# Output product of the attention half by token block, and the half weights of the last feed-forward output asked for one by one

## The chip, the cores and the metric

The program runs on one core of one Trainium2 chip. The metric is the device time of one launch in microseconds (us); lower is better. The kernel before takes 2506.91 us as the median of three runs, 2506.32 to 2507.97.

## What is computed

One layer of a streaming encoder for 1088 tokens: 1024 of a new stream and 64 of a running one, model width 1024, all in float32. A feed-forward half step and a layer norm come first, then two attention branches from one projection, then the part that the change touches, then a second feed-forward half step and a layer norm:

```python
h = _layer_norm(alpha * x + 0.5 * _swiglu(x, ffn1_wi, ffn1_wo), ln1_g, ln1_b)
oa, ob, ga, gb, states = mixer(h)
ya = oa.reshape(b, t, WIDTH_A) @ w_branch_a
yb = ob.reshape(b, t, WIDTH_B) @ w_branch_b
mix = (jax.nn.sigmoid(ga) * ya + jax.nn.sigmoid(gb) * yb) @ w_out
h = _layer_norm(alpha * h + mix, ln2_g, ln2_b)
h = _layer_norm(alpha * h + 0.5 * _swiglu(h, ffn2_wi, ffn2_wo), ln3_g, ln3_b)
```

`w_out` is 1024 x 1024. Its product and the second layer norm are called the output stage below.

## The kernel before

**Tiles.** Features lie on the 128 partitions, tokens along the free axis, so the width of 1024 is eight feature tiles (`KT` = 8, index `d` or `k`). The tokens are three blocks of 384, 384 and 320 (`TB`, index `b`).

**Products in three.** Every operand is split into a high and a low float32r part, and a product of one feature tile is three matmuls (high by high, high by low, low by high; `mm3`, line 495). One product of the output stage is `(d, b)`: 8 input tiles times 3 = 24 matmuls into one PSUM bank.

**Weights.** A chunk of weights (here 128 x 1024, 512 KB: all that is needed for one `d`) is loaded by a DMA on the SP queue into one of two raw buffers (`wr`; `dma_upto`, line 382), and split (`split_next`, line 395): ACT copies the high part into a weight slot, then DVE, or POOL where the chunk carries the flag `pool`, subtracts it to give the low part. There are two slots, `w_s0` and `w_s1`. A slot is free again when the last matmul of its chunk is done; a raw buffer when the low part of its chunk is done, and then the load of the chunk after the next is issued. `add` (line 458) makes one job of a chunk: get the weights, split the next chunk ahead, run the products of the blocks that it is given, release.

**The output stage.** `to_out` (line 2394) allots the result tiles `Y2` (`y2_d`, all tokens of one feature tile). `out_of(d, b, w)` (line 2410) takes a tile of `h` that was loaded from memory (`ask_h`, line 2337, three ahead), runs the product, and DVE forms `y = alpha * h + product`; from the second `d` on a running sum `acc` over the feature tiles is kept (`add_up`, line 816; for the last block it lies in a tile named `c`). After `d` = 7 of a block `norm2` plans its layer norm (`layer_norm`, line 532): a matmul with ones gives the mean; DVE subtracts it from the eight `y` (eight rows `y<-y,b`, called centring here); ACT or DVE squares; DVE or POOL adds the squares (`lns`, `lnq`); matmuls of one column give the variance; ACT and DVE give `rstd`; transposes spread it over the partitions; DVE scales (eight rows `y<-y,lnp,b`); the bias is added; and ACT, DVE and POOL form the high and low parts of the factors of the second feed-forward half (`A11`, `A12`, and from the second half of the tokens `S3`, `A22`).

Before the change the jobs are: for each `d`, blocks 0 and 1; then for `d` = 0 to 6 block 2, with the flag `pool` on every other chunk; then `last_out` (line 2428) with `(7, 2)`, which also starts the loads of the second feed-forward half and plans the norm of block 2.

**What sets the order.** `Plan` (line 131) holds a model of each engine's time and emits the instructions of the vector engines in the order in which that model says they can start, while PE's order is that of the jobs, with the norm's matmuls put in between. Each engine then works strictly through its own list, and waits on semaphores where an operand is missing. So a row that is late holds up every row behind it on its engine.

**The last output of both feed-forward halves.** `last_outputs` (line 1269) multiplies the last four hidden tiles by eight half chunks `l0` to `l7` (`get_unit`, line 979, makes sure that the split of one is planned). Before the change all eight are asked for ahead of the first product.

All vector instructions have line 120 of the profile, because one wrapper issues them; rows are told apart by their tiles.

Of the kernel before, what the change touches and what calls it, by code (L numbers as in the profile page):

```python
# [34 lines left out]
KT = D // P  # L35
# [8 lines left out]
NF = DFF // P  # L44
# [286 lines left out]
def tile_trunk(ctx, tc, a):  # L331
# [92 lines left out]
    def get(i):  # L424
        while st["split"] <= i:
            split_next()
        w, t = hls[i]
        plan.until(lambda: t.end is not None)
        return w

    def ahead(i):

        while st["split"] <= min(i, len(chunks) - 1) and free_slot() is not None:
            split_next()

    def release(i):
        finished[i] = plan.t["pe"]
        hls.pop(i)
# [19 lines left out]
    def add(ap, fn, cols=1024, pool=False, blocks=(0, 1, 2)):  # L458
        c = len(chunks)
        chunks.append((ap, cols, pool))  # L460

        def run():
            w = get(c)
            ahead(c + 1)
            for b in blocks:
                fn(b, w)
            release(c)
        jobs.append(run)
# [347 lines left out]
    def add_up(ACC, Y, d, b, n, tmp):  # L816

        def add(e):
            if d == 1:
                ACC[b] = tmp.tile([P, 384], F32, name="acc", tag="acc", bufs=2)  # L820
            other = Y[0, b] if d == 1 else ACC[b]
            of(e).tensor_tensor(ACC[b][:, :n], other[:, :n], Y[d, b][:, :n], op=OP.add)
        if d:
            summed[b] = plan.task(adders(n), "acc", add, [summed[b]] if d > 1 else (), 2, None, [Y[d, b]])
# [55 lines left out]
    def add_ffn7(wi, wo, wl, G, gi, put, beside_it, last, end):  # L880
# [93 lines left out]
        def some():  # L974
            while G.hold and at.next < len(units):
                prepare()
        G.some = some

        def get_unit(kind, f):
            i = by[kind, f]  # L980
            while at.next <= i:
                prepare()
            plan.until(lambda: units[i].t.end is not None)
            return units[i]
# [5 lines left out]
        def wait(*tasks):  # L990
            plan.until(lambda: all(t.end is not None for t in tasks))
# [147 lines left out]
        def out_products(fs, d, b, w, off):  # L1139

            n = TB[b]
            p = bank("mm")
            mm3(p, w, [F[f].h[:, :, TO[b]:TO[b] + n] for f in fs], n, off)
            y = Y[d, b]
            if (d, 0, 0) not in touched:
                wait(*G.read[d])
                nc.vector.scalar_tensor_tensor(y, y, ALPHA, p[:, :n], op0=OP.mult, op1=OP.add)
            else:
                nc.vector.tensor_tensor(y, y, p[:, :n], op=OP.add)
# [119 lines left out]
        def last_outputs():  # L1269
            fs = list(range(NF - 4, NF))  # L1270
            wait(*(F[f].t[x, s] for f in fs for x in ("h1", "h2") for s in range(2)))
            last()
            st["solo"] = False
            some()
            us = [get_unit(f"l{d}", NF) for d in range(KT)]
            for b in range(3):
                if b:
                    G.next_weights()
                for d in range(KT):
                    wait(*(outs[d, half, s, 0] for half in range(1 + (b > 0)) for s in range(2)))  # L1280
                    skip = 2 * (d < 2)
                    out_products(fs[skip:], d, b, us[d].slot, skip)
                    if gi == 2 and b == 2:
                        last_norm(d, b, Y, ACC, G.tmp, G.room, put)
                    else:
                        add_up(ACC, Y, d, b, TB[b], G.tmp)
                    if b == 2:
                        G.freed(us[d].home)
                if gi < 2 or b < 2:
                    layer_norm(b, [Y[k, b] for k in range(KT)], ACC, gi, G.tmp, put, G.room(b) if gi == 2 else None)  # L1290
# [36 lines left out]
        for x, fs in order:  # L1327
            for f in fs:
                if x == "plain":
                    f, half = f  # L1330
# [34 lines left out]

        jobs.extend(steps)
        jobs.append(last_outputs)
        jobs.append(end)

# [950 lines left out]
    def fetch(order, tag, bufs, load):  # L2320

        order, ready = list(order), {}

        def ask(key):
            while key not in ready or (order and len(ready) < bufs):
                x = order.pop(0)
                n = TB[x[1]]
                ready[x] = load(x[0], x[1], n)
            return ready.pop(key)
        return ask  # L2330
# [3 lines left out]
        nc.sync.dma_start(h[:, :n], h_d[d * P:(d + 1) * P, TO[b]:TO[b] + n])  # L2334
        return h

    ask_h = fetch([(d, b) for d in range(KT) for b in (0, 1)] + [(d, 2) for d in range(KT)], "or", 3, load_h)

    gate_order = [(d, b) for d in range(6) for b in range(3)] + [(d, b) for b in range(3) for d in (6, 7)]
    GT, gated = {}, {}  # L2340
# [69 lines left out]
    def out_of(d, b, w):  # L2410
        n = TB[b]
        h = ask_h((d, b))
        p = bank("mm")
        mm3(p, w, have_m(b), n)
        nc.vector.scalar_tensor_tensor(Y2[d, b], h[:, :n], ALPHA, p[:, :n], op0=OP.mult, op1=OP.add)
        add_up(ACC2, Y2, d, b, n, G2.tmp if b < 2 else Own)

    def norm2(b, tmp):
        layer_norm(b, [Y2[k, b] for k in range(KT)], ACC2, 1, tmp, put2)

    def f_out(d):
        def fn(b, w):
            out_of(d, b, w)
            if d == KT - 1:
                norm2(b, G2.tmp)
        return fn
# [57 lines left out]
        add(*br[d], cols=512)  # L2484
    add_joint(br[6:], cols=512)
    jobs.append(to_out)
    for d in range(KT):
        add(a["wout"][d], f_out(d), blocks=[0, 1])
    for d in range(KT - 1):
        add(a["wout"][d], f_out(d), blocks=[2], pool=d % 2 == 0)  # L2490
    chunks.append((a["wout"][KT - 1], 1024, False))
    jobs.append(last_out)

# [132 lines left out]
```

## Time and profile before

| | us |
|---|---|
| median of the runs | 2506.91 |
| the profiled execution | 2507.51 |
| its span, first to last instruction | 2505.7 |
| PE busy in the span | 2432.4 |
| PEld (weight loads into the array) busy | 2379.4 |
| DVE busy | 1752.6 |
| ACT busy | 1285.1 |
| POOL busy | 349.0 |

The output stage runs from 1639.9 us to 1748.1 us of the span, the norm of its last block to 1773 us. A row of a timeline gives the start, the time that it took, the engine, the tiles it writes and reads, how many instructions are merged in it, and in brackets how long the engine had been idle before it and what ended that. PEld is the clearest engine for gaps of TensorE: before each matmul its weights go into the array, and while PE is kept busy PEld is too. A granted clock (PEclk) of 1.00 is 2.4 GHz and 0.50 is 1.2 GHz.

### The profile page before, as it was taken

How to read it: one execution, taken by the hardware profiler on the slowest of the kernel's cores; microseconds unless marked ns; L12 is line 12 of the kernel's file. 1: busy time of each engine (PE TensorE's matmuls, PEld its weight loads, DVE VectorE, ACT ScalarE, POOL GpSimd, SP SyncE). 2: the span in 40 equal slices, each digit the busy share in tenths (PEclk: the TensorE clock that was granted, in tenths of full speed). 3: DMA queues.
4: the chain of work that ended last, by engine and by line, in shares of the span. 5: the costliest groups of instructions: out<-in, count | busy, mean ns of one | idle time of the engine just before them, and what ended most of it. 6: DMA issues, size and time to landing. Idle time of an engine off the chain costs nothing.

```text
span 2505.7 us, 46746 instructions
## 1 busy us (share of the span) xinstructions
PE 2432.4 (97%) x17338; PEld 2379.4 (95%) x17338; DVE 1752.6 (70%) x4246; ACT 1285.1 (51%) x2712; POOL 349.0 (14%) x477
## 2 busy tenths in 40 slices
PE   9999999999999999999999999999999999999995
PEld 9999999999998899999999998998999999999995
DVE  7666655666586889888676767657956665667758
ACT  5333333333345698777857777524633333343324
POOL 0000000000042222222243332314000000000004
PEclk9999999999999999999999999999999999999997
DMA  5466532273222322223221111643256643145322
GB/s 184 125 207 204 170 103 88 86 222 93 81 84 89 117 70 86 92 76 92 68 77 54 60 51 55 200 139 117 79 151 190 189 145 91 60 141 189 90 67 72
DMA packets 221204, 285.41 MB, mean 114 GB/s; under 512 B 20704, under 2 KB 146512, under 8 KB 220944
## 3 DMA queue, kind: packets, MB, share of 16 engines
q1 hardware_dynamic: 200864, 257.40, 33.4%
q10 hardware_dynamic: 19552, 22.81, 2.8%
q8 instruction: 136, 2.23, 0.4%
q0 software_dynamic: 560, 2.21, 0.2%
q14 instruction: 92, 0.75, 0.1%
HBM read 207.62 MB, written 75.00 MB: 113 GB/s over the span
## 4 chain that ended last, share of the span: by engine, by line
PE 76%; DVE 9%; ACT 8%; issue 3%; DMA 3%; POOL 1%; ACTq 0%; SPq 0%; DVEq 0%; POOLq 0%
PE b L120 76%; ACT w L120 2%; ACT scores L120 2%; DVE w L120 1%; DVE y L120 1%; DVE k L120 1%; ACT pt L120 1%; DMA g<-g_d 1%; DVE pt L120 1%; DVE scores L120 1%; DVE w_s L120 1%; ACT z L120 1%; DVE sc L120 0%; ACTq L120 0%; DMA st<-in_wo_dram 0%
## 5 line engine op out<-in xcount | busy, mean ns | idle before, releaser
L120 PE MATMUL b<-x,w_s 128*128 128x384 f32 (+1 forms) x3528 | 637.3, 332 | 6.3 <-ACT w_s L120 2.2
L120 PE MATMUL b<-A,w_s 128*128 128x272 f32 (+1 forms) x4824 | 633.1, 291 | 4.9 <-DVE y L120 1.8
L120 PEld LDWEIGHTS b<-A,w_s 128*128 128x128 f32 x4824 | 619.9, 189 | 9.4 <-ACT fac L120 2.1
L120 PEld LDWEIGHTS b<-x,w_s 128*128 128x128 f32 x3528 | 587.8, 189 | 15.2 <-ACT w_s L120 2.8
L120 PE MATMUL b<-S,w_s 128*128 128x272 f32 x4032 | 516.8, 288 | 3.0 <-ACT c L120 3.0
L120 PEld LDWEIGHTS b<-S,w_s 128*128 128x128 f32 x4032 | 509.0, 188 | 6.1 <-ACT c L120 4.4
L120 ACT ACTIVATE w_s<-wr 128x512 fp32r<-128x512 f32 (+1 forms) x345 | 227.4, 660 | 383.0 <-PE b L120 207.1
L120 DVE TENSOR_TENSOR w_s<-wr,w_s 128x512 fp32r<-128x512 f32 (+1 forms) x323 | 229.9, 714 | 143.8 <-ACT w_s L120 139.3
L120 PE MATMUL b<-fac,w_s 128*128 128x272 f32 x1800 | 228.2, 288 | 0.9 <-DVE y L120 0.9
L120 PEld LDWEIGHTS b<-fac,w_s 128*128 128x128 f32 x1800 | 226.8, 188 | 1.2 <-ACT fac L120 1.2
L120 POOL TENSOR_TENSOR w_s<-wr,w_s 128x256 fp32r<-128x256 f32 x196 | 149.6, 789 | 417.7 <-ACT w_s L120 170.5
L120 ACT ACTIVATE c<-b 128x272 f32<-128x272 f32 (+1 forms) x262 | 102.1, 391 | 97.2 <-PE b L120 88.9
L120 DVE TENSOR_TENSOR c<-c,b 128x272 f32<-128x272 f32 x240 | 103.4, 433 | 63.8 <-PE b L120 60.6
L120 POOL TENSOR_TENSOR lns<-lns,lnq 128x384 f32<-128x384 f32 (+1 forms) x25 | 27.1, 1084 | 739.2 <-ACT lnq L120 738.1
L120 DVE TENSOR_TENSOR pt<-b,pt 128x512 fp32r<-128x512 f32 (+4 forms) x184 | 96.5, 545 | 31.2 <-ACT pt L120 29.4
L120 POOL TENSOR_TENSOR y<-y,c 128x384 f32<-128x384 f32 (+1 forms) x15 | 17.3, 1174 | 706.0 <-DVE acc L120 691.3
L120 ACT ACTIVATE c<-c 128x272 f32<-128x272 f32 x160 | 69.0, 432 | 82.8 <-DVE c L120 80.4
L120 PE MATMUL b<-pt,v 128*128 128x256 f32 (+3 forms) x672 | 103.5, 281 | 4.9 <-DVE pt L120 2.3
L120 PEld LDWEIGHTS b<-pt,v 128*128 128x128 f32 (+1 forms) x672 | 93.5, 188 | 13.5 <-DVE pt L120 4.3
L120 ACT ACTIVATE w<-w,mx 128x640 f32<-128x640 f32 (+5 forms) x144 | 100.5, 698 | 10.4 <-DVE mx L120 7.6
L120 PE MATMUL b<-m,w_s 128*128 128x384 f32 (+1 forms) x576 | 100.4, 334 | 3.2 <-DVE w_s L120 2.6
L120 ACT ACTIVATE w<-w,sm 128x640 f32<-128x640 f32 (+5 forms) x144 | 97.7, 698 | 9.5 <-DVE sm L120 4.8
(274 smaller groups left out, 3235.5 us busy)
## 6 DMA issues: line engine op xcount, KB each, us to landing
wr<-in_wi_dram SPq DMA_DIRECT2D x156, 256.0 KB, 3.1
ff_d<-c SPq DMA_DIRECT2D x144, 136.0 KB, 2.9
a<-ff_d SPq DMA_DIRECT2D x72, 272.0 KB, 3.8
st<-in_wo_dram SPq DMA_DIRECT2D x72, 256.0 KB, 5.1
tw_d<-st SPq DMA_DIRECT2D x72, 256.0 KB, 2.6
wr<-in_wz_dram SPq DMA_DIRECT2D x35, 512.0 KB, 3.6
wr<-tw_d SPq DMA_DIRECT2D x48, 256.0 KB, 2.7
q<-in_wi_dram SPq DMA_DIRECT2D x39, 256.0 KB, 3.2
```

The source lines that it names most:

```text
L120: r = real(*args, **kw)
```

## The change

The output stage now goes by token block: all eight `d` of block 0, then all of block 1, then seven of block 2 and `last_out`. Each chunk of `w_out` is therefore loaded and split three times, 24 chunks in place of 16, and none of them carries the flag `pool` any more. The loads of `h` follow the new order. In `last_outputs` each half chunk is asked for just ahead of its first product.

```diff
@@ last_outputs
-            us = [get_unit(f"l{d}", NF) for d in range(KT)]
+            us = {}
             for b in range(3):
                 if b:
                     G.next_weights()
                 for d in range(KT):
+                    if not b:
+                        us[d] = get_unit(f"l{d}", NF)
                     wait(*(outs[d, half, s, 0] for half in range(1 + (b > 0)) for s in range(2)))
@@ the loads of h
-    ask_h = fetch([(d, b) for d in range(KT) for b in (0, 1)] + [(d, 2) for d in range(KT)], "or", 3, load_h)
+    ask_h = fetch([(d, b) for b in range(3) for d in range(KT)], "or", 3, load_h)
@@ the jobs of the output stage
     jobs.append(to_out)
-    for d in range(KT):
-        add(a["wout"][d], f_out(d), blocks=[0, 1])
-    for d in range(KT - 1):
-        add(a["wout"][d], f_out(d), blocks=[2], pool=d % 2 == 0)
+    for b in range(3):
+        for d in range(KT - (b == 2)):
+            add(a["wout"][d], f_out(d), blocks=[b])
     chunks.append((a["wout"][KT - 1], 1024, False))
     jobs.append(last_out)
```

What stands on the engines shows what moves. First PE, at the mean of block 0's norm (`acc..,ones`), before the change and then after it. The tiles `m0` to `m7` are the inputs, their second number is the block, `w_s0` and `w_s1` are the slots.

```order
L120 MATMUL b2_19926<-m2_1_19085,w_s0_19824 128x384 x3
L120 MATMUL b2_19926<-m3_1_19141,w_s0_19824 128x384 x3
L120 MATMUL b5_19940<-acc_19550,ones_132 128x384
L120 MATMUL b2_19926<-m4_1_19198,w_s0_19824 128x384 x3
L120 MATMUL b2_19926<-m5_1_19322,w_s0_19824 128x384 x3
```

```order
L120 MATMUL b0_19721<-m2_1_19085,w_s1_19684 128x384 x3
L120 MATMUL b0_19721<-m3_1_19141,w_s1_19684 128x384 x3
L120 MATMUL b5_19739<-acc_19524,ones_132 128x384
L120 MATMUL b0_19721<-m4_1_19198,w_s1_19684 128x384 x3
L120 MATMUL b0_19721<-m5_1_19322,w_s1_19684 128x384 x3
```

Before, this mean stands inside the last product of block 1 (the 16th product of the stage); now it stands inside the first product of block 1 (the 9th), so that norm has 15 products behind it where it had 8. The mean of block 1 stands in the first product of block 2 in both.

Next the SP queue behind the fourth chunk, before and after. `wr` is a chunk of weights, `h32` a tile of `h`.

```order
L120 DMA wr_19450<-in_wout_dram 128x1024
L120 DMA h32_19479<-h_d_71 128x384
L120 DMA h32_19509<-h_d_71 128x384
L120 DMA wr_19523<-in_wout_dram 128x1024
L120 DMA h32_19541<-h_d_71 128x384
```

```order
L120 DMA wr_19450<-in_wout_dram 128x1024
L120 DMA h32_19480<-h_d_71 128x384
L120 DMA wr_19495<-in_wout_dram 128x1024
L120 DMA h32_19514<-h_d_71 128x384
L120 DMA wr_19530<-in_wout_dram 128x1024
```

In blocks 0 and 1 each tile of `h` now has a chunk of weights ahead of it in the queue, where every second one had; in block 2 it was one to one already.

Last DVE, from the `y` of the last product `(7, 2)` towards the centring of block 2 (`y2_0<-y2_0,b5 128x320`), before and after. Rows of 160 and 384 columns belong to the norm of block 1.

```order
L120 SCALAR_TENSOR_TENSOR y2_7_19427<-h32_20218,b0_20309 128x320
L120 CAST A11_19428<-y2_0_19420 128x160
L120 TENSOR_TENSOR c_18677<-c_18677,y2_7_19427 128x320
L120 TENSOR_TENSOR A11_19428<-y2_0_19420,A11_19428 128x160
L120 TENSOR_TENSOR A11_19428<-y2_1_19421,A11_19428 128x160
L120 SCALAR_TENSOR_TENSOR y2_2_19422<-y2_2_19422,lnp_133,b7_20344 128x384
L120 SCALAR_TENSOR_TENSOR y2_3_19423<-y2_3_19423,lnp_133,b7_20344 128x384
L120 SCALAR_TENSOR_TENSOR y2_4_19424<-y2_4_19424,lnp_133,b7_20344 128x384
L120 CAST A11_19428<-y2_2_19422 128x160
L120 SCALAR_TENSOR_TENSOR y2_5_19425<-y2_5_19425,lnp_133,b7_20344 128x384
```

```order
L120 SCALAR_TENSOR_TENSOR y2_7_19427<-h32_20280,b0_20370 128x320
L120 CAST A12_19432<-y2_6_19426 128x160
L120 TENSOR_TENSOR c_18677<-c_18677,y2_7_19427 128x320
L120 TENSOR_TENSOR A12_19432<-y2_6_19426,A12_19432 128x160
L120 TENSOR_TENSOR A12_19432<-y2_7_19427,A12_19432 128x160
L120 TENSOR_TENSOR S3_20423<-y2_0_19420,S3_20423 128x224
L120 TENSOR_TENSOR w_s0_20429<-wr_20361,w_s0_20429 128x512 x2
L120 TENSOR_TENSOR S3_20423<-y2_1_19421,S3_20423 128x224
```

Between that `y` and the first centring row there are 26 instructions before the change and 14 after it. The 12 that are gone from there (six scalings, three low parts and two casts of 160 columns, one bias row) now stand ahead of the last product.

## Rows read from the trace of the kernel before

**Rows 1.** The page, part 1: busy us, share of the span and instructions of each engine.

```profile
PE 2432.4 (97%) x17338; PEld 2379.4 (95%) x17338; DVE 1752.6 (70%) x4246; ACT 1285.1 (51%) x2712; POOL 349.0 (14%) x477
```

**Rows 2.** Windows: stretch, length, busy PE, PEld, DVE, ACT, POOL, clock, DMA.

```profile
1641.00:1706.00 65.00, 64.94 (x369) 64.94 (x370) 27.31 (x43) 9.70 (x12) 4.72 (x6) 1.00 0.39 119
1706.00:1748.00 42.00, 36.82 (x229) 34.72 (x227) 38.02 (x67) 23.44 (x41) 22.22 (x23) 0.96 0.46 149
1748.00:1773.00 25.00, 20.67 (x135) 19.36 (x136) 20.00 (x52) 16.55 (x38) 1.54 (x3) 0.86 0.25 75
```

**Rows 3.** Timeline of PEld over the output stage and behind it.

```profile
1718.34 0.74 PEld L120 LDWEIGHTS b<-ones,lns 128*128 128x128 f32 x6 [1.70 <-POOL lns L120]
...
1733.31 6.75 PEld L120 LDWEIGHTS b<-m,w_s 128*128 128x128 f32 x46 [1.59 <-DVE w_s L120]
1740.94 0.30 PEld L120 LDWEIGHTS b<-m,w_s 128*128 128x128 f32 x2 [0.88 <-ACT w_s L120]
1742.20 0.59 PEld L120 LDWEIGHTS b<-m,w_s 128*128 128x128 f32 x4 [0.96 <-DVE w_s L120]
...
1745.77 0.30 PEld L120 LDWEIGHTS b<-ident,rstd 128*128 128x128 f32 x3 [0.55 <-issue]
...
1748.07 0.42 PEld L120 LDWEIGHTS b<-A,w_s 128*128 128x128 f32 x3 [1.13 <-ACT y L120]
...
1762.93 0.79 PEld L120 LDWEIGHTS b<-A,w_s 128*128 128x128 f32 x6 [1.53 <-ACT c L120]
1766.76 1.23 PEld L120 LDWEIGHTS b<-ones,lns 128*128 128x128 f32 x6 [3.04 <-issue]
```

**Rows 4.** Windows of 4 us, same columns, where the clock is below 1.00.

```profile
1720.00:1724.00 4.00, 4.00 (x19) 4.00 (x18) 3.86 (x8) 3.11 (x6) 0.53 (x1) 0.57 0.67 184
...
1764.00:1768.00 4.00, 1.21 (x6) 1.22 (x6) 3.56 (x8) 2.27 (x3) 0.00 (x0) 0.60 0.41 110
1768.00:1772.00 4.00, 4.00 (x20) 4.00 (x20) 0.30 (x2) 0.40 (x2) 0.00 (x0) 0.54 0.28 91
```

**Rows 5.** Timeline of DVE in block 2 and behind it.

```profile
1707.14 2.41 DVE L120 TENSOR_TENSOR y<-y,b 128x384 f32<-128x384 f32 x5 [1.61 <-PE b L120]
...
1731.23 2.02 DVE L120 TENSOR_TENSOR w_s<-wr,w_s 128x1024 fp32r<-128x1024 f32 x1
...
1740.92 1.23 DVE L120 TENSOR_TENSOR w_s<-wr,w_s 128x1024 fp32r<-128x1024 f32 x1 [1.15 <-ACT w_s L120]
...
1747.47 0.48 DVE L120 SCALAR_TENSOR_TENSOR y<-h,b 128x320 f32<-128x320 f32 x1
...
1748.89 1.66 DVE L120 SCALAR_TENSOR_TENSOR y<-y,lnp,b 128x384 f32<-128x384 f32 x3
...
1757.48 0.48 DVE L120 TENSOR_TENSOR y<-y,b 128x320 f32<-128x320 f32 x1
```

**Rows 6.** Instructions on the tile m: weight loads into the array.

```profile
L120 PEld LDWEIGHTS b<-m,w_s x576: 186/188/329, 1639.9 to 1746.7; 128*128 128x128 f32 x192
```

**Rows 7.** Timelines of ACT and SP: one split, and the load issued when it ended.

```profile
1649.47 1.06 ACT L120 ACTIVATE w_s<-wr 128x1024 fp32r<-128x1024 f32 x1 [3.72 <-PE b L120]
...
1651.82 0.33 SPq L120 DMA_DIRECT2D wr<-in_wout_dram  x1
```

**Rows 8.** The last chunk of the stage: its load's issue, ACT's row, and the load's landing.

```profile
1733.29 0.33 SPq L120 DMA_DIRECT2D wr<-in_wout_dram  x1
...
1739.83 1.06 ACT L120 ACTIVATE w_s<-wr 128x1024 fp32r<-128x1024 f32 x1 [1.55 <-DMA wr<-in_wout_dram]
...
DMA to landing us min/median/max: 6.5/6.5/6.5
```

**Rows 9.** DMA issues from 1640 to 1773 us: count, size, median us to landing.

```profile
wr<-in_wout_dram SPq DMA_DIRECT2D x16, 512.0 KB, 3.6
```

**Rows 10.** Last output of the second feed-forward half: the last half chunk on ACT and PE.

```profile
2430.30 0.63 ACT L120 ACTIVATE w_e<-wr 128x512 fp32r<-128x512 f32 x1 [2.77 <-DMA wr<-in_wl_dram]
...
2438.25 1.20 PE L120 MATMUL b<-h,w_e 128*128 128x384 f32 x6
```

## The prediction

> **What bounds the kernel now.** I read the page first: PE is busy for 97% of the span, so time can come only from the few places where TensorE stands still or runs at half clock [rows 1]. The windows by stage show where that is around the change. While blocks 0 and 1 are multiplied, PEld is busy 64.94 us of 65.00 and DVE 27.31: PE sets the pace, and DVE has room for more than as much again. In the 42 us in which block 2 is multiplied beside the norms of blocks 0 and 1, DVE is busy 38.02 and PEld only 34.72. In the 25 us behind, PEld is busy 19.36 [rows 2]. So the two norms that end together, at the end of block 1, crowd DVE, and TensorE pays.
>
> The timeline of PEld names the gaps [rows 3]. 1.70 us ahead of the variance matmuls of block 0's norm (`lns` came late from POOL, which at that time also did low parts of weights). 1.59 for a weight slot on DVE. 0.88 and 0.96 for the last chunk. 0.55 at the spreading of `rstd` of block 1. 1.13 for a factor of the second half. Then, behind the stage, 1.53 for ACT (`c`), and 3.04 ahead of the variance matmuls of block 2's norm. Their sum is 11.38 us. The clock adds to it: after the 1.70 gap it is 0.57 over 4 us, which with PE busy throughout costs 4 x 0.43 = 1.7. After the 3.04 gap it is 0.54 from 1768 to 1772, 4 x 0.46 = 1.8, and 0.50 for the 1.2 us before that in which PE worked, 0.6: together 2.4 [rows 4]. So 15.5 us lie in reach, 0.6% of the kernel. After 1773 PE goes on without such gaps, and what is won there stays won to the end.
>
> **The change part by part.** *Removed, 1.70 + 1.7.* Block 0's norm now begins in the first product of block 1. In that block DVE has eight centrings and eight `y<-h` at 0.48 each, eight scalings at 0.55 [rows 5], eight low parts of weights at 1.23 [rows 5], seven low parts of factors and ten additions at about 0.5 (my estimate from centrings of the same width), small rows of 1.3: 3.8 + 3.8 + 4.4 + 9.8 + 8.5 + 1.3 = 31.6 us. PE takes eight products of 24 x 0.1755 = 4.2 us (64.94 us for 370 loads [rows 2]), 33.7, plus 1.5 for the norm's own matmuls. It fits, tightly. And POOL, whose late row ended this gap, has lost the low parts of four chunks that stood between its additions. I take the whole gap, and the clock with it.
>
> *Removed, 1.59 + 0.55.* Before, block 2 carried centrings and scalings of two norms; now of one: by the same prices 3.8 + 3.8 + 4.4, seven low parts 8.6, and about 7 for the rest, 27.6 us beside 28.2 of products (24 x 0.147 = 3.5 each: 6.75 us for 46 loads [rows 3]) and 1.6 of other matmuls. Bounds: nothing of the two waits goes (DVE is still nine tenths full), or all. I take all, since the slot then has time: from ACT's start on a chunk to the load that waits for its low part are 2.35 us [rows 7], and a product lasts 3.5 or 4.2.
>
> *Removed in part, 0.9 of 1.84.* The last chunk was late for its load: issued at 1733.29, it took 6.5 us where the median is 3.6 [rows 8, 9], for the first loads of the feed-forward half follow it at once. They still do. But it is issued when the low part of the chunk two before is done, which stood just at the start of that chunk's product (PE went on at 1733.31 [rows 3]) and should now stand about 0.9 us ahead of it: 3.5 of a product less the 2.35 above and some 0.25 for two semaphores (my estimate). I take 0.9, between 0 and 1.84.
>
> *Removed, 1.53 + 3.04 + 2.4.* From the `y` of the last product to the first centring of block 2 DVE took 10.0 us, 1747.47 to 1757.48. Twelve of its 26 rows now stand earlier: six scalings, 3.3 us at 0.55 [rows 5], and six small rows that I estimate at 1.5. The centring comes 4.8 us earlier, at 1752.7 by this trace's time, and 9.3 us after it (1757.48 to 1766.76) the variance can begin: 1762.0. PE, without the two gaps, comes to it at 1766.76 - 3.04 - 1.53 = 1762.2. So both gaps go, by a hair, and PE itself is late next. The 1.53 wait is for ACT, whose row `c` stands behind squares of the same norm, which come earlier too. I take both, and the half clock after them. Bounds: 0 and 7.0.
>
> *Kept.* The 1.13 gap: the factors of block 1's last columns depend on a norm that still starts in the first product of block 2.
>
> *Added: eight chunks.* Eight loads of 512 KB on SP, eight ACT rows of 1.06 [rows 7], and twelve low parts on DVE, eight new and four that came from POOL. In block 0 they are hidden by the idle DVE of [rows 2]; in blocks 1 and 2 they are in the sums above. If the cover is gone, each is 1.23 us, or 2.02 beside a busy POOL [rows 5], on the way to the next product. SP waits with each load for a low part, and behind it stands a tile of `h`: its product's `y` would be late, and with it a PSUM bank, but there are five banks and three tiles of `h` ahead. In blocks 0 and 1 a chunk and a tile of `h` per 4.2 us are 704 KB, 170 GB/s; the same two kinds of load already went one to one in block 2, 672 KB per 3.5 us.
>
> *Weights used for one block only.* TensorE loads weights into its array 576 times for the stage's 24 x 24 = 576 matmuls [rows 6], so no load into the array is shared between blocks, before or after, and this costs 0. The Trainium skill, "TensorE: Matmul & The Clock Gate", section "Step-by-step: what each phase is for", speaks against the change: weights usually stay put over many matmuls, to be loaded once and used repeatedly. If loads were shared between two blocks here, splitting them would add 8 chunks x 16 loads x 188 ns = 24 us by the duration of [rows 6] where nothing hid them; the row's count says that there is nothing to lose.
>
> *Half chunks asked for one by one.* The products of the last outputs start without a gap before and after; only DVE's order changes, and two low parts per feed-forward half go to POOL. The last half chunk's ACT row starts at 2430.30; even if POOL took 2.02 us for its low part, the longest here for twice the width [rows 5], it would be done by 2433, and its product begins at 2438.25 [rows 10]. The tail of the kernel waits for additions of block 2, which keep their order. I take 0, bounds -0.5 and +0.5, the price of one low part of half width either way.
>
> **The sum.** 1.70 + 1.7 + 1.59 + 0.55 + 0.9 + 1.53 + 3.04 + 2.4 = 13.4 us. The profiled execution took 2507.5 (span 2505.7 and 1.8 around it), 0.6 above the median of 2506.9. So 2494.1 for that execution, and **2493.5 us** against the median.
>
> **The rivals.** *The tail stays* (0.10). If PE's gaps behind the stage were set by something other than the moved rows, say ACT, the 7.0 us remain: 2500.5. For it: ACT was busy 16.55 of the 25 us. Against it: DVE had hardly an idle moment from 1706 to 1768.
>
> *The waits come back at the switches* (0.12). Of the seven chunk switches in block 2 three had waits, 3.43 us in all, 0.49 per switch. With the 15 switches beside a norm each paying 0.49, 7.35 us return, of which 0.9 is already counted, and with two drops of the clock at 1.7 nearly all of the rest is gone but some 3.5: about 2503. For it: DVE nine tenths full. Decides: a low part that ends over 1 us late, as behind a DVE row next to a busy POOL.
>
> *The raw buffers become the bound* (0.05), the slower side. Two raw buffers allow two products per cycle of load, high part, low part. With the median landing the cycle is about 3.6 + 2.35 = 6.0 us, well below 2 x 3.5. But the last load needed 6.54 to ACT's row [rows 8]. If all took that, with low parts at 2.02 the cycle were 6.54 + 2.35 + 0.8 = 9.7, 4.85 per product: 16 x 0.65 + 8 x 1.35 = 21.2 lost against 13.4 won, 2514.7. It decides from a cycle of 9.1 us. Against it: of 16 loads the median is 3.6 [rows 9]. The same page of the Trainium skill, section "HAM oscillation — how this bites in real kernels", describes a kernel in which each weight tile's work is shorter than the wait for the next one and the clock falls at every tile. Here 24 falls at 1.7 would bring 41 us more, about 2556; I give that 0.01 of the 0.05, for in this trace the 1.59 gap for weights was followed by no fall.
>
> **How the numbers follow.** The forecast has 0.73, the three rivals 0.10, 0.12 and 0.05. About 0.2%, 5 us, can be told from no change. The forecast and the tail rival are faster by more, 0.83; the switches make no difference, 0.12; the raw buffers are slower, 0.05. For the range: if all 15.5 us went, and 0.5 at the half chunks, 2490.9, with the spread of the runs 2490; at the other end the tail rival, and the switches with two thirds of their price, 2502. That leaves out the slower case and part of the switches' on one side, and little on the other.
>
> **What would show it.** In the profile after: PEld without a gap over 0.5 us in blocks 0 and 1; no variance matmul that waits for `lns`; the clock at 1.00 through the stage and the 25 us behind it; the first centring of block 2 some 5 us after the last `y`; the first matmul on `A` about 102 us after the first on `m`, where it was 108 (1639.9 to 1748.07 [rows 3, 6]). Gaps that end on `w_s` or on a load of `w_out` in blocks 0 and 1 would show the forecast wrong, and so would DVE work that is still crowded at the end of block 2.

## The result and the profile after

The changed kernel takes 2496.03 us as the median of six runs (2489.62 to 2496.86); the kernel before, run on the same occasions, 2507.44 (2504.24 to 2509.81). The medians are 11.4 us apart; the ratio over all runs is 0.9949, 95% interval 0.9936 to 0.9962, by which the change saves about 12.8 us, between 9.5 and 16.0. The forecast was 2493.5, in the range 2490 to 2502. The profiled execution took 2496.86 us with a span of 2494.8, 10.9 shorter than that of before.

The page, part 1, of the changed kernel, with the columns of [rows 1]:

```profile
PE 2427.4 (97%) x17338; PEld 2375.3 (95%) x17338; DVE 1764.0 (71%) x4252; ACT 1297.6 (52%) x2725; POOL 339.5 (14%) x462
```

DVE and ACT have more work than before (11.4 and 12.5 us, most of it the extra splits), POOL less, and PE the same instructions in 5.0 us less. Where this comes from is shown by the windows, cut at 1706 as before, at the first product on `A`, and at 1773, to be read beside [rows 2]:

```profile
1641.00:1706.00 65.00, 64.70 (x371) 64.07 (x370) 48.32 (x75) 28.49 (x40) 6.52 (x7) 1.00 0.57 175
1706.00:1742.00 36.00, 36.00 (x239) 35.46 (x237) 32.80 (x57) 20.69 (x37) 6.24 (x7) 1.00 0.61 185
1742.00:1773.00 31.00, 30.02 (x234) 29.36 (x234) 28.08 (x69) 22.13 (x48) 0.00 (x0) 1.00 0.36 109
```

DVE's work has moved forward: 48.32 us in the first 65 us, where it was 27.31. PEld is full there all the same, and the stretch in which it was busy 34.72 of 42.00 has become one of 35.46 of 36.00. The clock is 1.00 in all three; over 4 us at a time from 1640 to 1792 it is never lower.

The timeline of PEld, beside [rows 3]:

```profile
1643.05 35.50 PEld L120 LDWEIGHTS b<-m,w_s 128*128 128x128 f32 x202 [0.62 <-DVE w_s L120]
1678.54 0.36 PEld L120 LDWEIGHTS b<-acc,ones 128*128 128x128 f32 x2
...
1690.27 0.81 PEld L120 LDWEIGHTS b<-ones,lns 128*128 128x128 f32 x6
...
1728.82 0.78 PEld L120 LDWEIGHTS b<-ones,lns 128*128 128x128 f32 x6
...
1742.68 0.42 PEld L120 LDWEIGHTS b<-A,w_s 128*128 128x128 f32 x3 [0.95 <-ACT y L120]
...
1756.63 0.73 PEld L120 LDWEIGHTS b<-ones,lns 128*128 128x128 f32 x6 [0.47 <-issue]
...
1760.41 0.13 PEld L120 LDWEIGHTS b<-ident,rstd 64*128 64x128 f32 x1 [0.17 <-issue]
```

Behind the wait for the first chunk's low part (0.62) there is no gap until the first product on `A`: the variances of blocks 0 and 1 (`ones,lns`) find their sums ready. Of 1.53 and 3.04 us behind the stage 0.47 is left.

The timeline of DVE, beside [rows 5]: one low part in block 1, the `y` of the last product, and the first centring of block 2.

```profile
1705.31 1.22 DVE L120 TENSOR_TENSOR w_s<-wr,w_s 128x1024 fp32r<-128x1024 f32 x1
...
1742.08 0.48 DVE L120 SCALAR_TENSOR_TENSOR y<-h,b 128x320 f32<-128x320 f32 x1
...
1747.34 0.48 DVE L120 TENSOR_TENSOR y<-y,b 128x320 f32<-128x320 f32 x1
```

The last two rows are 5.3 us apart, where they were 10.0. The loads of the weights into the array are 576 again, as in [rows 6], and the loads of `w_out` are 24, none of which anything waited for; the longest landing on record is 4.6 us. For the last chunk, whose load took 6.5 before [rows 8], the profile after has no landing, since nobody waited for it. Two answers on these tiles:

```profile
L120 PEld LDWEIGHTS b<-m,w_s x576: 186/188/192, 1642.1 to 1741.5; 128*128 128x128 f32 x192
```

```profile
DMA to landing us min/median/max: 3.6/3.7/4.6
```

**Where the time went.** I measure the stage from the first weight load on `m` to the last row of the spread of block 2's norm (64 rows of `ident,rstd`; 1772.67 before, 0.3 behind the row that my expectations below use). Before: 1772.67 - 1639.9 = 132.8. After: 1760.41 - 1642.1 = 118.3. So 14.5 us were won in the stage, 7.6 up to the `y` of the last product (107.6 after the first load, now 100.0) and 6.9 behind it. The span won only 10.9, for two reasons that lie outside. The first load on `m` comes 2.2 us later, 1642.1 for 1639.9, since PE waited 3.22 us for a chunk of the branch stage, 2.07 before, and the half clock behind it (0.52 and 0.53 from 1630.4 to 1634.0) cost about 1 us more. And behind the stage, at 2223, 96 weight loads took 13.59 us, 12.08 before. I put neither down to the order: in the twelve profiles of this study that leave the part ahead of the stage as it was, the first load lies anywhere from 1638.1 to 1644.1, and the 96 loads are slow in seven of all thirteen, in both orders (last section).

### The profile page after: what moved, and what is told of

Same layout as the page of the kernel before. It is cut to its first block, busy times and chain, and to the rows that moved or that the text cites. A ratio compares the mean times of both kernels' runs of the same rounds, so it can differ in the third digit from the quotient of the medians.

```text
span 2494.8 us, 46770 instructions
## 1 busy us (share of the span) xinstructions
PE 2427.4 (97%) x17338; PEld 2375.3 (95%) x17338; DVE 1764.0 (71%) x4252; ACT 1297.6 (52%) x2725; POOL 339.5 (14%) x462
## 4 chain that ended last, share of the span: by engine, by line
PE 79%; DVE 8%; ACT 7%; issue 2%; DMA 2%; POOL 1%; ACTq 0%; SPq 0%; DVEq 0%; POOLq 0%
PE b L120 79%; ACT w L120 2%; ACT scores L120 2%; DVE y L120 1%; DVE w L120 1%; DVE k L120 1%; ACT pt L120 1%; DVE pt L120 1%; DVE w_s L120 1%; ACT z L120 1%; DVE x L120 1%; DVE scores L120 0%; ACTq L120 0%; DMA st<-in_wo_dram 0%; SPq L120 0%
## 5 line engine op out<-in xcount | busy, mean ns | idle before, releaser
L120 ACT ACTIVATE w_s<-wr 128x512 fp32r<-128x512 f32 (+1 forms) x354 | 237.4, 672 | 364.4 <-PE b L120 205.7
L120 DVE TENSOR_TENSOR w_s<-wr,w_s 128x512 fp32r<-128x512 f32 (+1 forms) x335 | 246.1, 737 | 141.0 <-ACT w_s L120 135.8
L120 POOL TENSOR_TENSOR w_s<-wr,w_s 128x256 fp32r<-128x256 f32 x180 | 135.9, 782 | 354.2 <-DVE w_s L120 136.6
L120 PEld LDWEIGHTS b<-pt,v 128*128 128x128 f32 (+1 forms) x672 | 93.6, 188 | 13.5 <-DVE pt L120 4.1
L120 ACT ACTIVATE fac<-a 128x544 fp32r<-128x544 f32 x73 | 48.1, 659 | 104.9 <-PE b L120 88.5
L120 POOL TENSOR_TENSOR w_i<-wr,w_i 128x256 fp32r<-128x256 f32 (+1 forms) x9 | 7.9, 896 | 692.7 <-ACT w_i L120 692.7
```

The source lines that it names most:

```text
L120: r = real(*args, **kw)
```

## The experiments

The theory is that of the forecast: two norms that begin one product apart crowd DVE, PE pays in waits, and with the blocks one after the other DVE has room. The rivals: POOL's low parts were the trouble; the half chunks have a part; only block 0's norm was in the way; the loads or raw buffers bound it. Each run's stage is measured as above, in its one profile; "delay" is from the `y` of the last product to the first centring of block 2. The kernel before was run again beside each experiment, and the ratio is to those runs. The profile of e6 is of its longest execution, 2516.3 us, 7.3 above its median; part of that lies outside the stage (first load on `m` at 1644.1, the 96 loads slow).

| run | chunks | stage, us | delay, us | median, us | ratio to before (95%) |
|---|---|---|---|---|---|
| before | 16 | 132.8 | 10.0 | 2507.4 | |
| the change | 24 | 118.3 | 5.3 | 2496.0 | 0.9949 (0.9936 to 0.9962) |
| e1, half chunks only | 16 | 132.2 | 10.0 | 2509.9 | 1.0002 (0.9993 to 1.0012) |
| e2, order only | 24 | 118.3 | 5.3 | 2493.9 | 0.9946 (0.9933 to 0.9958) |
| e3, before without POOL's flag | 16 | 135.9 | 18.6 | 2510.5 | 1.0011 (1.0002 to 1.0020) |
| e4, the change with POOL's flag | 24 | 118.1 | 4.7 | 2499.1 | 0.9958 (0.9945 to 0.9970) |
| e5, halfway | 20 | 126.9 | 12.4 | 2503.5 | 0.9985 (0.9976 to 0.9994) |
| e6, blocks 1 and 2 together | 17 | 135.4 | 20.3 | 2509.1 | 1.0010 (1.0001 to 1.0019) |
| e7, two more DVE rows per `y` | 24 | 142.3 | 22.4 | 2517.4 | 1.0039 (1.0026 to 1.0051) |
| e11, one more DVE row per `y` | 24 | 133.2 | 14.8 | 2508.8 | 1.0002 (0.9993 to 1.0011) |
| e8, load placed later | 24 | 118.7 | 5.3 | 2493.0 | 0.9940 (0.9925 to 0.9955) |
| e9, one raw tile | 24 | 170.7 | 4.7 | 2545.8 | 1.0151 (1.0137 to 1.0165) |
| e10, gates planned later | 24 | 119.0 | 5.3 | 2493.6 | 0.9945 (0.9932 to 0.9959) |

### The parts of the change: e1 and e2

e1 is the first hunk of the diff alone, e2 the other two.

> Only the half chunks of the two feed-forward halves are asked for one by one; the output stage is as before. The forecast's theory (everything comes from the order of the token blocks) expects no difference: 2507 us, within 1 us of the kernel before (its term was 0, bounds 0.5 either way). A rival, that part of the 11 us comes from the half chunks, expects 2 us or more below the kernel before, and the span from the last outputs to the end shorter by as much.

> Only the output stage goes by token block, without the flag for POOL; the half chunks are asked for as before. The forecast's theory expects all of the gain: 2496 us, and from the first weight load on m to the spread of block 2's norm 118 us, where it was 132.5 before and 118.0 after the whole change. If the half chunks had a part, it is above 2497.5.

e1 makes no difference that the runs can tell (its interval goes from 1.8 us less to 3.0 more), e2 has all of the gain. The profiles are finer for the second feed-forward half: from the spread of block 2's norm to the end of the span the change takes 734.4 us and e2, without the half chunks, 734.3, both with slow 96 loads. So no cost or gain of the half chunks is seen, as forecast, and the order is the cause.

e1 showed one thing besides. Its stage is that of before with the same 1.70 wait, but this time the clock did not fall behind it. PEld, and the window of 4 us behind the wait:

```profile
1718.92 0.74 PEld L120 LDWEIGHTS b<-ones,lns 128*128 128x128 f32 x6 [1.70 <-POOL lns L120]
```

```profile
1720.00:1724.00 4.00, 4.00 (x31) 3.99 (x30) 3.96 (x9) 3.68 (x7) 0.50 (x1) 1.00 0.66 173
```

Before, the window behind that wait had the clock at 0.57 [rows 4]. The 24 loads on `m` behind the variance, in the kernel before and in e1:

```profile
1719.00 5.06 PEld L120 LDWEIGHTS b<-m,w_s 128*128 128x128 f32 x24
```

```profile
1719.58 3.53 PEld L120 LDWEIGHTS b<-m,w_s 128*128 128x128 f32 x24
```

They took 1.53 us less in e1. Yet e1 came to its first product on `A` only 1.1 us sooner (107.1 us after the first load on `m`, 108.2 before), and 0.26 of this is the wait for the first chunk's low part, 0.62 for 0.88. So in the old order at most some 0.9 of the 1.5 were PE's to win: without the fall it waits longer further on, since DVE is no faster. In the changed kernel those waits are gone too.

### POOL or the order: e3 and e4

```diff
 e3, on the kernel before
-        add(a["wout"][d], f_out(d), blocks=[2], pool=d % 2 == 0)
+        add(a["wout"][d], f_out(d), blocks=[2])
 e4, on the changed kernel
-            add(a["wout"][d], f_out(d), blocks=[b])
+            add(a["wout"][d], f_out(d), blocks=[b], pool=b == 2 and d % 2 == 0)
```

> The order of before (16 chunks), with the flag for POOL taken away: all low parts of w_out go to DVE. The forecast's theory (two norms crowd DVE at the end of block 1) expects no gain: the 1.70 us wait for POOL's sum and the half clock behind it (1.7) may go, but four low parts of 1.23 us, 4.9 us, come onto a DVE that was busy 38.0 of 42 us in block 2, and come out behind the stage: 2504 to 2510, the stage to block 2's spread 129 to 136 us. The rival, that POOL's low parts were the trouble and the order does not matter, expects most of the gain without the order: 2500 or less, the stage 124 us or less.

> The changed kernel with the flag for POOL on every other chunk of block 2 as before the change (16 low parts of 256 columns, 0.75 us each on POOL, beside one norm now). The forecast's theory expects most of the gain to stay, since only one norm lies beside them: 2496 to 2500, at most one wait for a sum on POOL of 1 to 2 us, with or without a fall of the clock (1.7). The rival, that POOL's low parts were the trouble, expects the waits of before to come back: 2500 to 2505.

Both stages came out as the theory says; e3's median lies 0.5 us above the upper end that I expected. In e3 the wait for POOL's sum is gone, and so is the half clock behind it, but the work that POOL had done came out behind the stage; PEld at the variance of block 1's norm:

```profile
1745.49 1.36 PEld L120 LDWEIGHTS b<-ones,lns 128*128 128x128 f32 x6 [6.27 <-issue]
```

In e4 POOL does 16 low parts again, and the stage is as short as without. Its median is 3.0 us above that of the change; the two intervals overlap, so I read nothing into it. POOL's late row, which ended the largest gap of block 2 in the kernel before, was how the crowding showed and not its cause.

### How far apart: e5 and e6

```diff
 e5, on the changed kernel
+    for d in range(4):
+        add(a["wout"][d], f_out(d), blocks=[0, 1])
     for b in range(3):
-        for d in range(KT - (b == 2)):
+        for d in range(4 if b < 2 else 0, KT - (b == 2)):
             add(a["wout"][d], f_out(d), blocks=[b])
 e6, on the changed kernel
-    for b in range(3):
-        for d in range(KT - (b == 2)):
-            add(a["wout"][d], f_out(d), blocks=[b])
+    for d in range(KT):
+        add(a["wout"][d], f_out(d), blocks=[0])
+    for d in range(KT):
+        add(a["wout"][d], f_out(d), blocks=[1, 2][:1 + (d < KT - 1)])
```

The order of the loads of `h` follows in both.

> Between the two orders: feature tiles 0 to 3 for blocks 0 and 1 together, then 4 to 7 for block 0, then 4 to 7 for block 1, then block 2: 20 chunks. Block 0's norm has 12 products behind it (8 before the change, 15 after), block 1's norm begins 4 products after it. The theory (two norms crowd DVE) by rows of the changed kernel: the two norms take some 12 us of DVE each (31.6 and 27.05 us busy in blocks 1 and 2, less 16 products at 2.1 for y, sum and low part), so from the 12th product on DVE has 12 x 2.1 + 24.6 = 50 us of work where PE has some 48. DVE is over-full by a little: part of the gain is lost, stage (first weight load on m to the spread of block 2's norm) 120 to 127 us where it was 132.8 before and 118.3 after, time 2497 to 2504. The rival, that any start of block 0's norm a few products ahead of block 1's is enough, expects the stage at 118 to 119 and the time of the changed kernel, 2496 or, with four low parts fewer, less.

> Block 0 alone, then for each feature tile blocks 1 and 2 (17 chunks). Block 0's norm is far from any other, but the norms of blocks 1 and 2 now begin one product apart at the end of the stage, with no product behind them. The theory expects that crowding two norms costs wherever it is: about a norm's chain of work (14 us from the first centring to the first factor) with little for PE beside it, stage 130 to 145 us, time 2508 to 2523. The rival, that only the norm of block 0 was in the way, expects the gain to stay: stage 121 us or less, 2499 or less.

e5 keeps some 4 of the 11 us: with four products between the norms the waits among the products are gone (its last `y` comes 99.0 us after the first load on `m`), but the delay behind it is 12.4 us, and PEld has the whole tail of before again:

```profile
1757.38 0.80 PEld L120 LDWEIGHTS b<-A,w_s 128*128 128x128 f32 x6 [1.88 <-ACT c L120]
1761.23 1.23 PEld L120 LDWEIGHTS b<-ones,lns 128*128 128x128 f32 x6 [3.05 <-issue]
```

Next e5's window from the start of the 13th product to the end of the products, and those of the delay, in e5 and in the change:

```profile
1691.00:1739.00 48.00, 48.00 (x307) 47.46 (x305) 43.44 (x72) 28.59 (x44) 12.69 (x13) 1.00 0.55 179
1739.50:1752.00 12.50, 11.20 (x79) 10.23 (x80) 11.21 (x29) 9.36 (x25) 2.61 (x5) 1.00 0.21 77
```

```profile
1742.00:1747.40 5.40, 4.69 (x35) 4.49 (x35) 5.27 (x17) 5.08 (x14) 0.00 (x0) 1.00 0.42 137
```

Beside the products DVE is busy 43.44 us of 48. That is no larger a share than in the blocks of the changed kernel (below), so it doesn't tell the two apart. What came out behind the products does: 11.2 us of DVE's work ahead of the first centring, 5.3 in the change.

In e6 block 0's norm is as free as in the change, and the gain is lost all the same: a wait of 7.50 us ahead of block 1's variance, and a delay of 20.3. So it is not block 0's norm as such: two norms that begin close together near the end cost as much when they are those of blocks 1 and 2.

### How much room DVE has left: e7 and e11

```diff
 e7 (two) and e11 (one), on the changed kernel, ahead of each y
+        for _ in range(2 * (b > 0)):
+            nc.vector.tensor_tensor(h[:, :n], h[:, :n], h[:, :n], op=OP.max)
         nc.vector.scalar_tensor_tensor(Y2[d, b], h[:, :n], ALPHA, p[:, :n], op0=OP.mult, op1=OP.add)
```

> The changed kernel with two more DVE instructions ahead of each y in blocks 1 and 2 (a maximum of the tile of h with itself, which leaves it as it is; 0.5 us each, 16 us in all). The theory says that DVE is nearly full there, 31.6 of 35.5 us in block 1 and 27.05 of 30 in block 2, so that 16 us are some 9 more than there is room for: waits on w_s, lns or rstd come back, most of the gain is lost, stage 125 to 132 us, 2503 to 2510. The rival, that PE was held up before by something else than DVE (ACT, POOL or the loads) and DVE's share only looked tight, expects 2 us at most: 2496 to 2498.

> One more DVE instruction ahead of each y in blocks 1 and 2 (0.5 us each, 8 us in all) where the run before had two. If the cost is work beyond the room (room 35.5 - 31.6 in block 1 and 30 - 27.05 in block 2, 6.9 us in all), it is 0 to 2 us: 2496 to 2498, no gap ahead of the variance of block 1's norm over 1 us. If, as the run with two suggests, y and low parts go ahead of the norm's rows, so that the norm of block 1 slides as a whole behind the last product and its chain lies bare there (12.5 us with 16 us more), the gap is 3 to 7 us already: 2500 to 2506.

The diff shows e7; e11 has one such row in place of two. That DVE is the bound holds; the sizes were misses, 21 us for e7 where I expected 7 to 14, and for e11 a time 2.8 us above the upper end of its range. The changed kernel's windows by block, on which the 6.9 us of room rest:

```profile
1676.00:1711.50 35.50, 35.50 (x205) 35.20 (x204) 31.61 (x53) 20.18 (x31) 5.07 (x5) 1.00 0.54 162
1711.50:1741.50 30.00, 30.00 (x206) 29.72 (x205) 27.05 (x47) 17.04 (x30) 5.22 (x6) 1.00 0.62 192
```

Part of the misses is that the rows were dearer than the 0.5 us that I had put down (0.64 at 384 columns and 0.59 at 320 in e11). The windows of the whole stage, in the change, in e11 and in e7:

```profile
1642.10:1760.40 118.30, 117.01 (x734) 115.27 (x732) 95.83 (x170) 61.72 (x104) 12.73 (x13) 1.00 0.56 170
```

```profile
1638.08:1771.25 133.17, 123.83 (x734) 120.48 (x732) 106.09 (x186) 61.19 (x102) 13.68 (x16) 0.95 0.48 151
```

```profile
1641.00:1783.30 142.30, 122.81 (x734) 119.94 (x732) 114.69 (x198) 62.16 (x104) 20.41 (x19) 0.93 0.44 141
```

DVE's busy time rose by 10.3 us in e11 and 18.9 in e7, not by 8 and 16, and the stage by 14.9 and 24.0. PEld of e7, then of e11, at the variance of block 1's norm:

```profile
1754.15 1.35 PEld L120 LDWEIGHTS b<-ones,lns 128*128 128x128 f32 x6 [12.54 <-issue]
```

```profile
1742.91 0.81 PEld L120 LDWEIGHTS b<-ones,lns 128*128 128x128 f32 x6 [3.37 <-issue]
...
1760.97 0.80 PEld L120 LDWEIGHTS b<-A,w_s 128*128 128x128 f32 x6 [0.93 <-ACT c L120]
1764.83 1.23 PEld L120 LDWEIGHTS b<-ones,lns 128*128 128x128 f32 x6 [3.05 <-issue]
```

The products hardly wait (one wait of 1.58 us in e7, four of 0.24 to 0.96 in e11): in DVE's order the `y` and the low parts that PE needs at once stand ahead of the norms' rows. It is the norms that slide. In e7 block 0's variance comes 61.1 us after the first load on `m`, 48.2 in the change; block 1's centring begins behind the last `y` (1745.30 for 1744.90), and its whole chain of centring, squares, sums and variance then lies bare, with nothing for PE to do. With that come the waits behind it and the half clock (0.53 from 1764.8 to 1771.2 in e11). Less the room of 6.9 us the added work leaves an excess of 3.4 us in e11 and 12.0 in e7, and the stage grew by 11.5 and 12.0 us more than that. So the price of too much work on DVE is the excess and, by these two points, a nearly constant 12 us, which I put down to the chain that is pushed behind the last product. With 10.3 us more the whole gain is gone: the changed kernel has room for less than that.

### The raw buffers: e8 and e9

```diff
 e8, on the changed kernel
-                dma_upto(i + NRAW)
+                dma_upto(i + (1 if i in st["one"] else NRAW))
 e9, the same and
-            r = wraw.tile([P, 1024], F32, name="wr", tag="wr")
+            r = st["raw"] if i - 1 in st["one"] else None
+            r = r or wraw.tile([P, 1024], F32, name="wr", tag="wr")
+            st["raw"] = r if i - 1 in st["one"] else None
```

> The changed kernel, but in the output stage a chunk's load is issued only when the low part of the chunk just before it is done, so that one raw buffer is in use where two were. The cycle of one buffer by the rows of before is 3.6 for the load and 2.35 from ACT's start to the end of the low part, 6.0 us, where a product takes 4.2 or 3.5: with 22 products on that cycle, 15 x 1.8 + 7 x 2.5 = 44 us more, stage about 162 us, time about 2540 if the clock stays up. If TensorE's clock falls at each of these waits of some 2 us (1.7 us each by the fall in the kernel before), up to 37 us more, 2577. If the loads had been what bounds the changed kernel anyway, it would be less than 20 us.

> The changed kernel, but from the second chunk of the output stage on every chunk is loaded into one and the same raw tile, so that its load has to wait for the low part of the chunk just before it (in the run before, only the place of the load in the program moved, its buffer was still free one chunk earlier, and the load could go as early as ever). The cycle of one buffer by rows is 3.7 for the load and 2.35 from ACT's start to the end of the low part, 6.0 us, where a product takes 4.2 or 3.5: over 22 products 15 x 1.8 + 7 x 2.5 = 44 us more, stage about 162, time about 2540 if the clock stays up; with a fall of 1.7 us at each wait up to 2577. A load that is faster when it is alone (the shortest landing was 3.6, for a quarter of the traffic it may be 3) would make it 2525. If the two raw buffers were not what gives the loads their time, it stays at 2496.

The lines that set `st["one"]` (the chunks of the stage) and the first value of `st["raw"]` are left out here. e8 did not test what I meant it to: it moved the load in the program, but the load still waited only for the buffer of the chunk before the last, and the kernel runs as the change does. e9 does test it, and the rival's cycle is now measured. One chunk on SP, then on ACT, then on DVE:

```profile
1656.11 0.33 SPq L120 DMA_DIRECT2D wr<-in_wout_dram  x1
...
1662.20 0.33 SPq L120 DMA_DIRECT2D wr<-in_wout_dram  x1
```

```profile
1659.85 1.06 ACT L120 ACTIVATE w_s<-wr 128x1024 fp32r<-128x1024 f32 x1 [5.03 <-DMA wr<-in_wout_dram]
```

```profile
1660.94 1.23 DVE L120 TENSOR_TENSOR w_s<-wr,w_s 128x1024 fp32r<-128x1024 f32 x1
```

Load to ACT 3.74, ACT to the end of the low part 2.32 (2.35 in [rows 7]), the next load 0.03 later: 6.09 us, for the 6.0 that the forecast worked out. Over two buffers that is 3.05 us per product, where a product takes 3.5 or 4.2. The loads hold nobody up in the changed kernel, and at this landing they have some 0.45 us per product to spare; with the longest landing of the change, 4.6 us, it would be next to nothing. The stage became 52.4 us longer, where 46.5 follow from a cycle of 6.09; part of the rest are falls of the clock in blocks 1 and 2.

In block 0 of e9 the clock did not fall at all:

```profile
1644.00:1692.00 48.00, 38.30 (x197) 33.54 (x195) 20.46 (x32) 9.99 (x12) 0.00 (x0) 1.00 0.37 121
```

Here PEld waits some 2 us at every chunk (1.03 for the high part, 0.96 for the low part), is busy 33.54 us of 48, and runs at full clock. In block 2 it fell behind waits that were little longer, 2.24 and 0.96 us with two loads between them:

```profile
1746.31 0.30 PEld L120 LDWEIGHTS b<-m,w_s 128*128 128x128 f32 x2 [2.24 <-ACT w_s L120]
```

```profile
1748.00:1752.00 4.00, 4.00 (x19) 4.00 (x19) 2.67 (x5) 2.83 (x5) 2.75 (x3) 0.58 0.55 172
```

The Trainium skill, "TensorE: Matmul & The Clock Gate", section "HAM oscillation — how this bites in real kernels", describes a kernel in which the wait for the next slice of an operand, some 3 to 5 us, is longer than the work on one slice, and in which the clock falls at every slice. The waits here are shorter than those: in block 0 this trace has none of the falls, and in block 2 some.

### A version beside both: e10

PE's wait for the last branch chunk, ahead of the stage, differs from run to run (1.03 to 3.22 us) and was the larger part of what the profile of the change lost outside the stage. On ACT that chunk's split stood behind a sigmoid that waited 2.02 us for its load.

```diff
 e10, on the changed kernel, in next_gate
-        t1 = plan.task("act", "sig", sig, (), 2, None, [g])
+        t1 = plan.task("act", "sig", sig, (), 2, None, [g], plan.dma + 1000)
```

> The changed kernel, with the sigmoids of the gates planned 1 us later than their load, so that on ACT the split of the last branch chunk stands ahead of the sigmoid that waited 2.02 us for its load; this is ahead of the output stage. In the changed kernel that split began at 1629.83 and PE waited 3.22 us for it (2.07 before the change, 1.03 to 2.89 in the other runs); it could begin at about 1627.1, so that the wait is under 1 us. Expected 1 to 3 us less than the changed kernel, with a fall of the clock behind the wait (1 to 1.5 us, in about half of the profiles) also gone: 2492 to 2495. The rival, that the sigmoids moved behind it make the tiles m late, expects the wait to come back at the next chunk or at the first product on m: 2496 or more.

PEld of e10 at that chunk, and where the first low part of `w_out` is awaited:

```profile
1627.90 9.51 PEld L120 LDWEIGHTS b<-x,w_s 128*128 128x128 f32 x58 [0.18 <-DVE w_s L120]
...
1639.11 1.00 PEld L120 LDWEIGHTS b<-m,w_s 128*128 128x128 f32 x6 [1.40 <-DVE w_s L120]
```

The wait of 3.22 us is 0.18, and 0.8 of it comes back at that low part, 1.40 for 0.62: theory and rival each have a part. The time is 2493.6 us, 0.9945 of before. That is faster than before, but its interval doesn't part it from the change, nor from e2; three of the four versions that hold the order and change little else lie between 2493.0 and 2493.9, and which of them is best stays open.

## Why the prediction was right, point by point

- **The bound.** That DVE's crowding in block 2 and behind cost PE its time is shown from both sides: taking the norms apart takes the waits away (e2), and putting 10.3 us of idle work on DVE brings the time of before (e11).
- **The sum of DVE's work.** 31.6 us for block 1 and 27.6 for block 2 were forecast from single rows; 31.61 and 27.05 were measured, in 35.5 and 30.0 us. That it agrees to a digit is partly luck: the `y<-h` of block 1 were put at 0.48 us from a row of 320 columns, and at 384 they took 0.55. "It fits, tightly" was right, and e11 shows how tightly.
- **1.70 + 1.7.** Both went. By the rows the half clock had cost 1.5 us (5.06 for 3.53, e1 above). It was right to count it only because the change took DVE's waits away with it: in e1, where the clock stayed up and DVE was as full as before, at most 0.9 was won. The forecast did not say this.
- **1.59 + 0.55.** Both went, the upper of the two bounds.
- **0.9 of 1.84.** Too small: the whole 1.84 went. The last load went out 8.65 us ahead of its product (1729.56; the product is the last 24 of 72 loads that take 10.56 us from 1731.17, so from 1738.2), 6.8 before (1733.29 [rows 8], and PE was free for it from 1740.94 - 0.88 = 1740.06 [rows 3]). That is 1.9 earlier, where I had worked out 0.9. ACT split the chunk 5.44 us behind its issue (1735.00), when its slot came free and not when the load landed.
- **1.53 + 3.04 + 2.4.** The first centring was forecast 5.2 us behind the last `y`, measured 5.3. Of 4.57 us of waits 0.47 is left, the half clock is gone.
- **Kept 1.13.** It is 0.95.
- **Added, eight chunks.** Hidden, as forecast: nobody waited for a load of `w_out`, and the low parts are in DVE's sums above. The array's loads stayed 576.
- **Half chunks.** 0 within what e1 and the profiles can tell.
- **What is won stays won.** After 1773 I saw no such gaps. There is one, of 2.05 us at 2235.76 (last section), and the profile of the change lost 1.5 us behind it by the clock.
- **The sum.** 13.4 forecast, 14.5 won in the stage. The last chunk's load gave 0.94 more; 0.45 came from two gaps behind the stage that I had left out (0.15 and 0.30, for factors from POOL), 0.26 from the first chunk's low part and 0.18 from the kept gap. The 0.47 that is left of the tail's waits goes off, and 0.44 for the two half clocks: they were 1.53 us and, by the time from the variance of block 2 to the last row of the spread (5.91 us before, 3.78 after), 2.13. That makes 14.3; the other 0.2 is not traced. The whole program shows 12.8 by the ratio, 13.5 in e2, each with some 3 us either way. The forecast time was 2.5 us too low, less than the spread of the runs.
- **The rivals.** The tail did not stay, no wait came back at the switches, the raw buffers don't bind (e9). What I had not named is the way in which it could have failed by little: 10 us more on DVE, and the norms would have slid behind the last product with hardly a wait at the switches.

## What to carry to other kernels

Where two long chains start close together and share a vector engine, add up that engine's rows for each stretch between their starts; if they fit when the starts are apart, loading weights again can be the cheaper side, provided that the array's loads were not shared anyway. Then look for what slides when they don't fit: rows that the next product needs go first, so the cost is not the excess alone but also the chain that it pushes behind the last product. And count half clock behind a wait as time to win only where the change also takes away the waits on the engine that set the pace; else most of it may come back as longer waits.

## What the runs showed of the hardware

The same wait may or may not make the clock fall. Behind the stage all thirteen profiles have one wait of 1.92 to 2.83 us, at the same instructions, followed by 96 weight loads. They took 12.06 to 12.09 us in six profiles and 13.59 to 13.61 in seven, and nothing between; over the first 4 us of them the granted clock was 1.00 in the kernel before and 0.61 in the change. PEld of the kernel before, and of the change:

```profile
2235.76 12.08 PEld L120 LDWEIGHTS b<-A,w_s 128*128 128x128 f32 x96 [2.05 <-ACT fac L120]
```

```profile
2223.49 13.59 PEld L120 LDWEIGHTS b<-A,w_s 128*128 128x128 f32 x96 [2.02 <-ACT w_s L120]
```

The length of the wait doesn't decide it: 2.57 us (e10) passed without a fall, 2.02 did not. What does was not found; a single profile carries 1.5 us of chance by this fall, and more by what comes ahead of the stage: 2.2 us by the one wait for the last branch chunk, 6 us by the first load on `m` as a whole. In the profile of the change the two together, 1.5 and 2.2 us, are the difference between the 14.5 us of the stage and the 10.9 of the span.
